# Attention by pairs of heads: probabilities times values on two halves of the array

## The chip, the cores and the metric

The kernel runs on one core of a Trainium2 chip. The metric is the time of one execution on the device in microseconds. The numbers of the profile come from one execution that the hardware profiler recorded. TensorE (PE) executes one queue in order: its matmuls appear as PE, its weight loads as PEld. VectorE is DVE, ScalarE is ACT, GpSimd is POOL, and SP issues the DMAs.

## The reference

Two layers work on 512 latent tokens and 256 context tokens, model width 1024. A layer is a half-step SwiGLU feed-forward, then four groups of heads side by side (a convolution, a linear recurrence, RWKV-7 in both directions, and attention), a joint output projection, and a second feed-forward half-step. Cut to the attention group, it computes this:

```python
def mla_mixer(u, uc, need_ctx_out, q_norm, w_uq, kv_norm, w_ukv, cos, sin):
    # q, k: 4 heads of 64 + 32 rotary columns; v: 4 heads of 64 columns
    k_all = jnp.concatenate([k, k_c], axis=1)      # 512 latent + 256 context keys
    v_all = jnp.concatenate([v, v_c], axis=1)
    def attend(q, k, v):
        s = jnp.einsum('bqhd,bkhd->bhqk', q, k, preferred_element_type=jnp.float32) * SM_SCALE
        p = jax.nn.softmax(s, axis=-1).astype(v.dtype)
        return jnp.einsum('bhqk,bkhd->bqhd', p, v)
    o = lax.map(lambda qb: attend(qb, k_all, v_all), q_blocks)   # blocks of 128 queries
    if need_ctx_out:
        o_c = attend(queries(uc), k_c, v_c)        # context attends to context alone
```

The last layer needs no context output.

## The kernel before

Everything is kept transposed, features on the 128 partitions and tokens along the free axis. The program is written as Python generators that emit instructions. A planner then orders each engine's queue: it takes instructions by priority (mostly the order in which they are emitted) as soon as its own model of time has their inputs ready, and less urgent work, above all the feed-forward matmuls of `gemm` (L503), fills what is left. The queues are fixed when the program is built; at run time each engine goes through its own in order and waits on semaphores. Tiles with one tag share a number of slots (`bufs`), and a slot is used again when the last reader of its old content is done.

`mla` (L886) emits the attention. It runs four times: for the context in layer 0 (`out` true, two blocks of 128 queries, two key tiles), for the latent tokens in layer 0 and in layer 1 (four blocks, six key tiles), and for the context in layer 1, where only keys and values are made. For each of four heads, one after the other, it makes the keys `kT` (L910 to L912, whose rotary part GpSimd copies) and the queries `qT` (L919 to L925); for each block of queries it makes the scores (L936, L938), the softmax (L941 to L945), the transposes of the probabilities in groups of three (L950), their copies into `pt` (L951), and the products with the values (L953), which are accumulated in one PSUM bank `po` for two heads: the even head writes partitions 0 to 63, the odd head 64 to 127. The tags `kT`, `qT` and `p` have two slots each, `pt` has one. After two heads, `split` (L514) writes `po` as the two parts that the output projection reads.

For the context and for the latent pass of layer 0, the steps of `mla` are dealt out alternately with those of `lru`, the linear recurrence (`merge`). In layer 1's latent pass attention runs as a whole beside the RWKV pipeline, and `lru` follows it. RWKV takes chunks through four stages: elements, the inverse of a triangular matrix in many small GpSimd instructions (L1171 to L1177), its composition from blocks (`rw_lev`), and the chain over chunks (`rw_chain`, L1242), which ends in readouts:

```python
for p, H in PH if need_y else []:      # H: partitions 0-63, then 64-127
    nc.tensor.matmul(py[H, p * 64:p * 64 + 64], sv[:, p, H], wr[:, p * 2 + c, 1, H], ...)      # L1279
for p, H in PH if need_y else []:
    nc.tensor.matmul(py[H, p * 64:p * 64 + 64], uv[H, p, H], lq[H, p * 2 + c, 1, :], ...)      # L1281
```

`rstd` (L418) spreads a column over 128 partitions; with two groups it goes through the two halves of the partitions in turn:

```python
for b in range(nb):
    for i in range(G):
        nc.tensor.matmul(ps[i * w:(i + 1) * w, b * 128:(b + 1) * 128], r[...].to_broadcast([128, w]), self.ident, ...)   # L435
```

Of the kernel before, what the change touches and what calls it, by code (L numbers as in the profile page):

```python
# [9 lines left out]
F32 = mybir.dt.float32  # L10
F32R = mybir.dt.float32r
AF = mybir.ActivationFunctionType
ALU = mybir.AluOpType
# [11 lines left out]
SM_SCALE = 96.0 ** -0.5  # L25
# [154 lines left out]
class Net:  # L180
# [705 lines left out]
    def mla(self, l, S, wp, yp, out, pr):  # L886
        nc, V, N = self.nc, self.nc.vector, S.n
        g = pr["g"]
        isx = S.i == 0
        nb = N // 128  # L890
        rp = self.c[:, C_RP:C_RP + 512]
        wkv = wp.tile([128, 4, 2, 64], F32, name=self.nm("wkv"))
        nc.sync.dma_start(out=wkv, in_=self.ins["ukv_w"][l])
        if out:
            wuq = wp.tile([128, 8, 128], F32, name=self.nm("wuq"))
            nc.sync.dma_start(out=wuq[:, :, 0:96], in_=self.ins["uq_w"][l].rearrange("p k h c -> p (k h) c"))
            self.rotcols(wuq[:, :, 64:128])

        vt = wp.tile([128, 4, 256], F32, name=self.nm("vt")) if isx else self.vtc
        for b in range(nb):  # L900
            ps = self.pM()
            nc.tensor.matmul(ps[:, 0:256], self.ckv[:, b * 128:(b + 1) * 128], wkv[:, :, 1, :], start=True, stop=True)
            nc.scalar.copy(out=vt[:, b, :], in_=ps[:, 0:256])
        vals = [vt[:, b, :] for b in range(nb)] + ([self.vtc[:, b, :] for b in range(2)] if isx else [])
        nk = len(vals)
        ys = []
        for h in range(4):
            kT = wp.tile([96, N], F32, tag="kT", name=self.nm("kT"), bufs=2) if isx else self.kTc[:, h, :]
            ps = self.pM()
            nc.tensor.matmul(ps[0:64, 0:N], wkv[:, h, 0, :], self.ckv, start=True, stop=True)  # L910
            nc.scalar.copy(out=kT[0:64], in_=ps[0:64, 0:N])
            nc.gpsimd.tensor_copy(out=kT[64:96], in_=self.kr)  # L912
            yield
            if not out:
                continue
            qT = wp.tile([96, N], F32, tag="qT", name=self.nm("qT"), bufs=2)
            ps = self.pM()
            for k in range(2):
                nc.tensor.matmul(ps[:, 0:N], wuq[:, k * 4 + h, :], self.cq[k], start=(k == 0), stop=(k == 1))  # L919
            if isx:  # L920
                nc.scalar.copy(out=qT[0:64], in_=ps[0:64, 0:N])
                t1 = wp.tile([128, nk * 128], F32, tag="p", name=self.nm("r1"), bufs=2)[:, 0:N]
                V.tensor_tensor(out=qT[64:96], in0=ps[64:96, 0:N], in1=rp[64:96], op=ALU.mult)
                V.tensor_tensor(out=t1[64:96], in0=ps[96:128, 0:N], in1=rp[96:128], op=ALU.mult)
                V.tensor_tensor(out=qT[64:96], in0=qT[64:96], in1=t1[64:96], op=ALU.add)  # L925
            else:
                nc.scalar.copy(out=qT, in_=ps[0:96, 0:N])
            n = nk * 128
            r = (h % 2) * 64
            if h % 2 == 0:  # L930
                po = self.pM() if self.wide else self.pC()
            for qb in range(nb):
                pt = wp.tile([128, nk, 128], F32, tag="pt", name=self.nm("pt"), bufs=1)
                ps = self.p2()
                q = qT[:, qb * 128:(qb + 1) * 128]
                nc.tensor.matmul(ps[:, 0:N], q, kT, start=True, stop=True)  # L936
                if isx:
                    nc.tensor.matmul(ps[:, N:n], q, self.kTc[:, h, :], start=True, stop=True)  # L938
                st = wp.tile([128, 4], F32, tag="st", name=self.nm("st"), bufs=4)
                p = wp.tile([128, n], F32, tag="p", name=self.nm("p"), bufs=2)  # L940
                V.tensor_reduce(out=st[:, 0:1], in_=ps[:, 0:n], axis=mybir.AxisListType.X, op=ALU.max)  # L941
                V.tensor_scalar(out=st[:, 1:2], in0=st[:, 0:1], scalar1=-SM_SCALE, scalar2=None, op0=ALU.mult)
                nc.scalar.activation(out=p, in_=ps[:, 0:n], func=AF.Exp, scale=SM_SCALE, bias=st[:, 1:2], accum_out=st[:, 2:3])
                V.reciprocal(out=st[:, 3:4], in_=st[:, 2:3])
                V.tensor_scalar(out=p, in0=p, scalar1=st[:, 3:4], scalar2=None, op0=ALU.mult)  # L945
                for k0 in range(0, nk, 3):
                    kn = min(3, nk - k0)
                    pp = self.pM()
                    for k in range(kn):
                        nc.tensor.transpose(pp[:, k * 128:(k + 1) * 128], p[:, (k0 + k) * 128:(k0 + k + 1) * 128], self.ident)  # L950
                    nc.scalar.copy(out=pt[:, k0:k0 + kn, :], in_=pp[:, 0:kn * 128].rearrange("p (k q) -> p k q", k=kn))  # L951
                for k in range(nk):
                    nc.tensor.matmul(po[r:r + 64, qb * 128:(qb + 1) * 128], vals[k][:, h * 64:(h + 1) * 64], pt[:, k, :], start=(k == 0), stop=(k == nk - 1))  # L953
                yield
            if h % 2:
                yt = self.ysplit(S, yp, 2)
                self.split(yt, po, N)
                ys.append(yt)
        self.my = ys


# [456 lines left out]
```

## Time and profile before

| | |
|---|---|
| median of three runs | 3392.51 us |
| lowest and highest of them | 3391.83, 3399.7 us |
| the profiled execution: its time, its span | 3401.43, 3399.7 us |
| mean granted clock of TensorE | 0.972 of full speed |
| attention, context, layer 0 | about 440 to 545 us |
| attention, latent, layer 0 | about 1040 to 1240 us |
| attention, latent, layer 1 | about 2730 to 2912 us |

A row of the chain of waits names an engine, a tile, a line and how many records were merged. An idle time is put down to the instruction that released the engine last. A tile's shape such as 128*64 after a matmul is that of its weights: 128 rows by 64 columns; behind it stands the moving tile.

### The profile page before, as it was taken

Reading aid. Unit: us, or ns where it says so; the run is one execution under the profiler, and the core shown is the slowest. Engines: PE = TensorE matmul, PEld = TensorE weight load, DVE = VectorE, ACT = ScalarE, POOL = GpSimd, SP = SyncE. Lnnn points to the kernel's source line nnn. Section 1 sums busy time; section 2 is a strip of 40 time slices with the busy share of each in tenths; the row PEclk is TensorE's granted clock in tenths of the full one; section 3 lists DMA queues with packets and bytes.
Section 4 is the critical chain, followed back from the end, with each engine's and each line's share of the span. In section 5 each row is a group of like instructions: output and inputs, shape, how many; then the busy total and the mean of one; then the engine's idle time right before and its main releaser. Section 6 shows DMA issues by size and latency. Waiting matters only on the chain.

```text
span 3399.7 us, 52623 instructions
## 1 busy us (share of the span) xinstructions
PE 3207.9 (94%) x20670; PEld 2598.6 (76%) x20670; DVE 2027.2 (60%) x3437; ACT 1383.2 (41%) x2364; POOL 961.9 (28%) x1205
## 2 busy tenths in 40 slices
PE   7999999999898999899999999999999889899998
PEld 3798866777776789688987778878888656578887
DVE  4555853554797565985676644543348977563335
ACT  3444553233536443444556332332235234642223
POOL 0222301351331123783212521211114266011111
PEclk9999999999999999899999999999999899899999
DMA  9665554432223454344544334233332251133232
GB/s 333 201 184 185 158 160 154 133 88 88 84 70 114 124 162 127 86 117 129 151 137 130 83 88 134 64 118 94 98 103 86 65 139 30 31 122 100 93 99 81
DMA packets 203544, 403.43 MB, mean 119 GB/s; under 512 B 97569, under 2 KB 103201, under 8 KB 203297
## 3 DMA queue, kind: packets, MB, share of 16 engines
q1 hardware_dynamic: 203296, 400.07, 38.8%
q8 instruction: 163, 2.67, 0.3%
q14 instruction: 85, 0.69, 0.1%
HBM read 392.39 MB, written 7.61 MB: 118 GB/s over the span
## 4 chain that ended last, share of the span: by engine, by line
PE 76%; DVE 13%; ACT 3%; issue 3%; DMA 2%; POOL 2%; SPq 0%; DVEq 0%; ACTq 0%; POOLq 0%
PE pg L503 60%; DVE ac L829 3%; PE pg L380 2%; PE pt L503 2%; DVE wlo L494 1%; PE pm L1119 1%; PE pm L380 1%; PE pt L936 1%; PE pc L953 1%; ACT whi L490 1%; DVE nacc L448 1%; PE pm L503 1%; POOL bt L1176 1%; PE pm L1220 1%; POOL bz L1177 1%
## 5 line engine op out<-in xcount | busy, mean ns | idle before, releaser
L503 PE MATMUL pg<-h,whi 128*128 128x256 f32 (+1 forms) x6128 | 1209.9, 345 | 17.8 <-ACT h L466 8.3
L503 PEld LDWEIGHTS pg<-h,whi 128*128 128x128 f32 x6128 | 976.1, 191 | 199.6 <-issue 30.3
L494 POOL TENSOR_TENSOR wlo<-raw,whi 128x1024 fp32r<-128x1024 f32 (+1 forms) x234 | 537.0, 2296 | 1997.4 <-ACT whi L490 1213.0
L490 ACT CAST whi<-raw 128x1024 fp32r<-128x1024 f32 (+1 forms) x621 | 607.3, 980 | 1073.5 <-PE pg L503 847.6
L494 DVE TENSOR_TENSOR wlo<-raw,whi 128x1024 fp32r<-128x1024 f32 (+1 forms) x387 | 449.7, 1163 | 403.6 <-PE pg L503 197.7
L503 PE MATMUL pg<-h,wlo 128*128 128x256 f32 (+1 forms) x3064 | 632.2, 344 | 6.7 <-DVE wlo L494 4.6
L503 PE MATMUL pg<-hid,whi 128*128 128x256 f32 (+1 forms) x2688 | 548.6, 340 | 19.6 <-DVE hid L517 5.4
L503 PEld LDWEIGHTS pg<-h,wlo 128*128 128x128 f32 x3064 | 492.0, 190 | 91.2 <-issue 16.3
L503 PEld LDWEIGHTS pg<-hid,whi 128*128 128x128 f32 x2688 | 425.8, 193 | 93.2 <-issue 11.2
L503 PE MATMUL pg<-hid,wlo 128*128 128x256 f32 (+1 forms) x1344 | 289.6, 334 | 3.0 <-POOL wlo L494 2.2
L522 DVE SCALAR_TENSOR_TENSOR x<-pg,msc,x 128x512 f32<-128x512 f32 (+1 forms) x232 | 155.2, 674 | 187.7 <-PE pg L503 186.5
L503 PEld LDWEIGHTS pg<-hid,wlo 128*128 128x128 f32 x1344 | 218.4, 193 | 27.9 <-POOL wlo L494 2.3
L517 DVE TENSOR_TENSOR hid<-ft,hid 128x512 fp32r<-128x512 f32 (+1 forms) x154 | 139.3, 905 | 60.7 <-ACT hid L516 60.3
L516 ACT CAST hid<-ft 128x512 fp32r<-128x512 f32 (+1 forms) x154 | 81.3, 528 | 220.9 <-DVE ft L552 220.6
L552 DVE SCALAR_TENSOR_TENSOR ft<-pg,ft 128x512 f32<-128x512 f32 (+1 forms) x152 | 86.8, 571 | 130.1 <-PE pg L503 129.2
L829 DVE SCALAR_TENSOR_TENSOR ac<-z,dw,ac 128x512 f32<-128x512 f32 (+1 forms) x180 | 142.2, 831 | 1.3
L551 DVE SCALAR_TENSOR_TENSOR ft<-ft,pg 128x512 f32<-128x512 f32 (+1 forms) x152 | 86.2, 567 | 90.9 <-ACT ft L550 90.5
L1177 POOL TENSOR_TENSOR bz<-bz,bt 32x14 f32<-32x14 f32 (+6 forms) x336 | 114.1, 340 | 23.8
L1176 POOL TENSOR_TENSOR bt<-bu,bz 32x14 f32<-32x14 f32 (+6 forms) x336 | 107.2, 319 | 22.9
L550 ACT ACTIVATE ft<-pg 128x512 f32<-128x512 f32 (+1 forms) x152 | 76.5, 503 | 71.5 <-PE pg L503 71.0
L522 DVE SCALAR_TENSOR_TENSOR ctx<-pg,msc,ctx 128x256 f32<-128x256 f32 x144 | 68.2, 480 | 49.4 <-PE pg L503 47.3
L466 ACT ACTIVATE h<-nt,mod 128x256 fp32r<-128x256 f32 x136 | 63.8, 503 | 74.7 <-DVE nt L465 74.4
(356 smaller groups left out, 3371.5 us busy)
## 6 DMA issues: line engine op xcount, KB each, us to landing
raw<-in_ffn_w_dram SPq DMA_DIRECT2D x456, 512.0 KB, 3.6
aw<-in_ada_w_dram SPq DMA_DIRECT2D x72, 512.0 KB, 5.6
raw<-in_ada_w_dram SPq DMA_DIRECT2D x72, 512.0 KB, 3.9
raw<-in_w_in_dram SPq DMA_DIRECT2D x65, 512.0 KB, 3.6
raw<-in_w_out_dram SPq DMA_DIRECT2D x56, 256.0 KB, 2.8
raw<-in_ffn_w_dram SPq DMA_DIRECT2D x40, 256.0 KB, 2.8
dl<-lq SPq DMA_DIRECT2D x48, 64.0 KB, 2.2
xt<-dz SPq DMA_DIRECT2D x48, 64.0 KB, 2.4
```

The source lines that it names most:

```text
L380: nc.tensor.matmul(pa[j * 32:(j + 1) * 32, :], self.cT[:, k, :], w[:, (j % 2) * 512:(j % 2) * 512 + 512], start=(k == 0), stop=(k == 7))
L490: nc.scalar.copy(out=hi[:, 0:n], in_=raw[:, 0:n])
L494: eng.tensor_tensor(out=lo[:, 0:n], in0=raw[:, 0:n], in1=hi[:, 0:n].bitcast(F32), op=ALU.subtract)
L503: self.nc.tensor.matmul(seg(ps[0:m, 0:N], s), W[w][:, k, c0:c0 + m], seg(hs[k][:, q, 0:N], s), start=(first and i == 0), stop=(last and i ...
L516: nc.scalar.copy(out=dst[:, 0, 0:N], in_=src[:, 0:N])
L517: nc.vector.tensor_tensor(out=dst[:, 1, 0:N], in0=src[:, 0:N], in1=dst[:, 0, 0:N].bitcast(F32), op=ALU.subtract)
L522: self.nc.vector.scalar_tensor_tensor(out=x, in0=seg(ps[:, 0:S.n], s), scalar=gate(m, S.i), in1=x, op0=ALU.mult, op1=ALU.add)
L551: nc.vector.scalar_tensor_tensor(out=t, in0=t, scalar=1.0, in1=pg[:, 0:N], op0=ALU.add, op1=ALU.mult)
L552: nc.vector.scalar_tensor_tensor(out=t, in0=pu[:, 0:N], scalar=0.5, in1=t, op0=ALU.mult, op1=ALU.mult)
L829: V.scalar_tensor_tensor(out=ac, in0=z, scalar=w, in1=ac, op0=ALU.mult, op1=ALU.add)
L1176: nc.gpsimd.tensor_tensor(out=tt, in0=u.u[:, I, k:k + 1].to_broadcast([32, n, m]), in1=z[:, k:k + 1, J].to_broadcast([32, n, m]), op=ALU.mult)
L1177: nc.gpsimd.tensor_tensor(out=z[:, I, J], in0=z[:, I, J], in1=tt, op=ALU.subtract)
```

## The change

The loop over four heads becomes a loop over two pairs. Keys and queries of both heads are made first. For each block of queries, both heads go through scores, softmax and transposes into a `pt` of their own (two slots), and then the products of the two heads alternate, key tile by key tile. The generator also yields after each head's transposes and after the products.

```diff
-        for h in range(4):
-            kT = wp.tile([96, N], F32, tag="kT", name=self.nm("kT"), bufs=2) if isx else self.kTc[:, h, :]
...
-            yield
-            if not out:
-                continue
-            qT = wp.tile([96, N], F32, tag="qT", name=self.nm("qT"), bufs=2)
...
+        for h0 in (0, 2):
+            kTs, qTs = [], []
+            for h in (h0, h0 + 1):
+                kT = wp.tile([96, N], F32, tag="kT", name=self.nm("kT"), bufs=2) if isx else self.kTc[:, h, :]
...
+                kTs.append(kT)
+                yield
+                if not out:
+                    continue
+                qT = wp.tile([96, N], F32, tag="qT", name=self.nm("qT"), bufs=2)
...
+                qTs.append(qT)
             if not out:
                 continue
-            r = (h % 2) * 64
-            if h % 2 == 0:
-                po = self.pM() if self.wide else self.pC()
+            po = self.pM() if self.wide else self.pC()
             for qb in range(nb):
-                pt = wp.tile([128, nk, 128], F32, tag="pt", name=self.nm("pt"), bufs=1)
...
+                pts = []
+                for h, kT, qT in zip((h0, h0 + 1), kTs, qTs):
+                    pt = wp.tile([128, nk, 128], F32, tag="pt", name=self.nm("pt"), bufs=2)
...
+                    pts.append(pt)
+                    yield
+
                 for k in range(nk):
-                    nc.tensor.matmul(po[r:r + 64, qb * 128:(qb + 1) * 128], vals[k][:, h * 64:(h + 1) * 64], pt[:, k, :], start=(k == 0), stop=(k == nk - 1))
+                    for r, pt in zip((0, 64), pts):
+                        h = h0 + r // 64
+                        nc.tensor.matmul(po[r:r + 64, qb * 128:(qb + 1) * 128], vals[k][:, h * 64:(h + 1) * 64], pt[:, k, :], start=(k == 0), stop=(k == nk - 1))
                 yield
-            if h % 2:
-                yt = self.ysplit(S, yp, 2)
-                self.split(yt, po, N)
-                ys.append(yt)
+            yt = self.ysplit(S, yp, 2)
+            self.split(yt, po, N)
+            ys.append(yt)
```

The instructions between (scores, softmax, transposes, copies) are the same as before, one loop deeper.

## Rows read from the trace of the kernel before

**Rows 1.** The page, part 1, busy us, share of the span and instructions.
```profile
PE 3207.9 (94%) x20670; PEld 2598.6 (76%) x20670; DVE 2027.2 (60%) x3437; ACT 1383.2 (41%) x2364; POOL 961.9 (28%) x1205
```

**Rows 2.** The page, part 4, shares of the chain that ended last, by engine.
```profile
PE 76%; DVE 13%; ACT 3%; issue 3%; DMA 2%; POOL 2%; SPq 0%; DVEq 0%; ACTq 0%; POOLq 0%
```

**Rows 3.** Windows: length, busy us (instructions) of PE, PEld, DVE, ACT, POOL; clock, DMA share, GB/s.
```profile
440.00:545.00 105.00, 103.11 (x463) 70.35 (x462) 44.41 (x95) 48.97 (x91) 9.57 (x4) 1.00 0.40 119
1040.00:1240.00 200.00, 192.63 (x1273) 153.23 (x1273) 121.83 (x187) 105.89 (x171) 30.95 (x14) 0.99 0.41 125
2730.00:2912.00 182.00, 166.83 (x1894) 112.37 (x1890) 127.93 (x317) 82.56 (x233) 106.10 (x292) 0.97 0.28 68
```

**Rows 4.** Instructions of L953: records, ns (min/median/max), first and last start.
```profile
L953 PE MATMUL pc<-pt,vt x128: 272/273/324, 1064.6 to 1236.3; 128*64 128x128 f32 x128
...
L953 PE MATMUL pg<-pt,vt x128: 272/273/323, 2754.1 to 2908.8; 128*64 128x128 f32 x128
...
L953 PE MATMUL pc<-pt,vtc x96: 272/273/323, 462.0 to 1236.8; 128*64 128x128 f32 x96
...
L953 PE MATMUL pg<-pt,vtc x64: 272/273/273, 2755.0 to 2909.2; 128*64 128x128 f32 x64
```

**Rows 5.** The chain in order of time, 2895 to 2930: start us, us, what.
```profile
2898.99 1.46 PE pg L953 x12
...
2902.25 0.59 PE pm L435 x8
2902.83 1.31 PE pg L953 x12
```

**Rows 6.** The chain in order of time, 1575 to 1600.
```profile
1595.98 0.38 PE pc L1275 x8
1596.37 0.23 PE pc L1279 x8
1596.60 0.38 PE pc L1281 x8
```

**Rows 7.** The chain in order of time, 440 to 545.
```profile
462.07 0.58 PE pc L953 x4
```

**Rows 8.** Timeline of TensorE, 1555 to 1563: start us, us, engine, line, operation, records.
```profile
1557.61 0.45 PE L1266 MATMUL pc<-w,xt 64*64 64x64 f32 x8
...
1560.65 0.45 PE L1275 MATMUL pc<-uv,bk 128*64 128x64 f32 x8
1560.93 0.40 PE L1279 MATMUL pc<-wr,su 128*64 128x64 f32 x8
```

**Rows 9.** Groups of instructions, 2730 to 2912: busy us, mean ns, idle before and releaser.
```profile
L1177 POOL TENSOR_TENSOR bz<-bz,bt 32x14 f32<-32x14 f32 (+6 forms) x112 | 32.9, 294 | 7.6
L1176 POOL TENSOR_TENSOR bt<-bu,bz 32x14 f32<-32x14 f32 (+6 forms) x112 | 31.8, 284 | 7.7
...
L951 ACT COPY pt<-pg 128x384 f32<-128x384 f32 x32 | 14.3, 480 | 15.0 <-PE pg L950 13.6 <-PE pg L953 1.3
```

**Rows 10.** Timeline of GpSimd, 2785 to 2800.
```profile
2793.14 0.86 POOL L912 COPY kT<-kr 32x512 f32<-32x512 f32 x1
```

**Rows 11.** TensorE's waits, 1040 to 1240: us in total, times, longest; first and last of six.
```profile
PE pt L936 <- DVE qT L925: 3.8, 3, 2.0
...
PE pg L503 <- DVE ctx L522: 0.2, 1, 0.2
```

**Rows 12.** Waits of all engines, 1043 to 1237.
```profile
ACT pt L951 <- PE pm L950: 15.9, 7, 5.4
```

**Rows 13.** The chain's shares by line, 1040 to 1240 and 2730 to 2912.
```profile
by line: PE pg L503 45.3%; PE pc L953 12.0%; PE pt L936 7.1%; PE pm L950 5.3%; PE pg L380 4.9%; PE pm L861 3.5%; PE pt L938 3.4%; PE pm L919 2.8%; DVE qT L925 2.5%; DVE wlo L494 1.2%; PE pm L910 1.2%; ACT whi L490 1.0%; DVE ti L867 1.0%; PE
...
by line: PE pg L953 9.9%; PE pt L936 6.2%; issue 6.0%; PE pm L1119 5.7%; PE pg L950 4.8%; PE pg L380 4.2%; PE pm L1220 3.3%; PE pg L919 3.1%; ACT p L943 2.7%; DVE bx L1109 2.6%; PE pt L938 2.6%; DMA aw<-in_ada_w_dram 2.4%; DMA xx<-dz 2.1%; 
```

**Rows 14.** TensorE's waits, 2730 to 2912, first and last of 18.
```profile
PE pg L380 <- DMA aw<-in_ada_w_dram: 3.7, 3, 1.9
...
PE pm L1119 <- POOL bz L1177: 0.2, 1, 0.2
```

More of the change, by code (lines that the diff above doesn't have):

```diff
@@ L906, in mla @@
         ys = []
-        for h in range(4):
-            kT = wp.tile([96, N], F32, tag="kT", name=self.nm("kT"), bufs=2) if isx else self.kTc[:, h, :]
[L909 to L912, printed above, removed]
-            yield
+        for h0 in (0, 2):
+            kTs, qTs = [], []
+            for h in (h0, h0 + 1):
+                kT = wp.tile([96, N], F32, tag="kT", name=self.nm("kT"), bufs=2) if isx else self.kTc[:, h, :]
+                ps = self.pM()
+                nc.tensor.matmul(ps[0:64, 0:N], wkv[:, h, 0, :], self.ckv, start=True, stop=True)
+                nc.scalar.copy(out=kT[0:64], in_=ps[0:64, 0:N])
+                nc.gpsimd.tensor_copy(out=kT[64:96], in_=self.kr)
+                kTs.append(kT)
[3 more added lines that the diff above has]
+                qT = wp.tile([96, N], F32, tag="qT", name=self.nm("qT"), bufs=2)
+                ps = self.pM()
+                for k in range(2):
+                    nc.tensor.matmul(ps[:, 0:N], wuq[:, k * 4 + h, :], self.cq[k], start=(k == 0), stop=(k == 1))
+                if isx:
+                    nc.scalar.copy(out=qT[0:64], in_=ps[0:64, 0:N])
+                    t1 = wp.tile([128, nk * 128], F32, tag="p", name=self.nm("r1"), bufs=2)[:, 0:N]
+                    V.tensor_tensor(out=qT[64:96], in0=ps[64:96, 0:N], in1=rp[64:96], op=ALU.mult)
+                    V.tensor_tensor(out=t1[64:96], in0=ps[96:128, 0:N], in1=rp[96:128], op=ALU.mult)
+                    V.tensor_tensor(out=qT[64:96], in0=qT[64:96], in1=t1[64:96], op=ALU.add)
+                else:
+                    nc.scalar.copy(out=qT, in_=ps[0:96, 0:N])
+                qTs.append(qT)
@@ L914, in mla @@
             if not out:
                 continue
-            qT = wp.tile([96, N], F32, tag="qT", name=self.nm("qT"), bufs=2)
[L917 to L927, printed above, removed]
@@ L928, in mla @@
             n = nk * 128
-            r = (h % 2) * 64
-            if h % 2 == 0:
-                po = self.pM() if self.wide else self.pC()
+            po = self.pM() if self.wide else self.pC()
             for qb in range(nb):
-                pt = wp.tile([128, nk, 128], F32, tag="pt", name=self.nm("pt"), bufs=1)
[L934 to L951, printed above, removed]
@@ new lines, in mla @@
+                pts = []
+                for h, kT, qT in zip((h0, h0 + 1), kTs, qTs):
+                    pt = wp.tile([128, nk, 128], F32, tag="pt", name=self.nm("pt"), bufs=2)
+                    ps = self.p2()
+                    q = qT[:, qb * 128:(qb + 1) * 128]
+                    nc.tensor.matmul(ps[:, 0:N], q, kT, start=True, stop=True)
+                    if isx:
+                        nc.tensor.matmul(ps[:, N:n], q, self.kTc[:, h, :], start=True, stop=True)
+                    st = wp.tile([128, 4], F32, tag="st", name=self.nm("st"), bufs=4)
+                    p = wp.tile([128, n], F32, tag="p", name=self.nm("p"), bufs=2)
+                    V.tensor_reduce(out=st[:, 0:1], in_=ps[:, 0:n], axis=mybir.AxisListType.X, op=ALU.max)
+                    V.tensor_scalar(out=st[:, 1:2], in0=st[:, 0:1], scalar1=-SM_SCALE, scalar2=None, op0=ALU.mult)
+                    nc.scalar.activation(out=p, in_=ps[:, 0:n], func=AF.Exp, scale=SM_SCALE, bias=st[:, 1:2], accum_out=st[:, 2:3])
+                    V.reciprocal(out=st[:, 3:4], in_=st[:, 2:3])
+                    V.tensor_scalar(out=p, in0=p, scalar1=st[:, 3:4], scalar2=None, op0=ALU.mult)
+                    for k0 in range(0, nk, 3):
+                        kn = min(3, nk - k0)
+                        pp = self.pM()
+                        for k in range(kn):
+                            nc.tensor.transpose(pp[:, k * 128:(k + 1) * 128], p[:, (k0 + k) * 128:(k0 + k + 1) * 128], self.ident)
+                        nc.scalar.copy(out=pt[:, k0:k0 + kn, :], in_=pp[:, 0:kn * 128].rearrange("p (k q) -> p k q", k=kn))
+                    pts.append(pt)
+                    yield
```

## The prediction

> **What bounds the kernel now.** I read the page's busy times first [rows 1], then the chain that ended last [rows 2], and then cut out the three stretches in which attention runs [rows 3]. TensorE is busy 94% of the span and is 76% of the chain, so the first question for any edit is how much TensorE issue time it takes away; the second is whether TensorE in that stretch was the engine that the others waited for. The stretches differ in this. In the context pass (440 to 545 us) TensorE is busy 103.1 of 105 us, and in layer 0's latent pass (1040 to 1240) 192.6 of 200: what attention leaves free is filled with feed-forward matmuls (L503). In layer 1's latent pass (2730 to 2912) it is 166.8 of 182, the filler is the RWKV pipeline, and GpSimd is busy 106 us there [rows 3].
>
> The matmuls that the change touches are those of L953, probabilities times values. Each matmul of the program is two records, since 416 records [rows 4] stand for 208 matmuls: 4 heads x 2 blocks x 2 key tiles = 16 in the context pass and 4 x 4 x 6 = 96 in each of two latent passes. All have 64 columns of weights and a moving tile of 128 columns.
>
> In the chain, which lays instructions end to end, 12 such records (one head, one block) take 1.46 us, but 1.31 us when they follow another group with 64-column weights [rows 5]. So a record costs 1.31 / 12 = 0.109 us, and entering the form costs 0.15 us. The same 0.15 us shows a second time: eight records of L1279 cost 0.23 us right behind L1275, while L1275, which enters the form, and L1281, which leaves it, take 0.38 us [rows 6]. The four records of a block in the context pass take 0.58 us [rows 7], which is 4 x 0.109 + 0.15.
>
> **What a pair on two halves costs.** The row nearest to the new form is L435: 64-column weights, 128 moving columns, consecutive matmuls on alternating halves of one bank. Eight records take 0.59 us [rows 5]; less the 0.15 that is 0.055 us a record, half of L953's. L1279 alternates as well, with a different moving tile for each half as the pair will have, and its 0.23 / 8 = 0.029 us for 64 columns is the same rate again [rows 6]. So two halves run side by side in this kernel already, whether they share the moving operand or not.
>
> A rule of the Trainium skill speaks against this: the page "TensorE: Matmul & The Clock Gate", Part 3 (packing small matmuls), says that a weight load overlaps a running matmul only where the row group differs, and both halves of a pair use all 128 rows. By that rule the pair would save nothing and the sum below would be zero. The 0.055 us of L435 disagrees with it, and I go by the row.
>
> **The change, part by part.**
>
> *Interleaved products.* Before, a pair of heads and a block cost 2 x 1.46 = 2.92 us; after, 24 x 0.055 + 0.15 = 1.47, so 1.45 less. A latent pass has 2 pairs x 4 blocks = 8 of these, 11.6 us; two passes give 23.2. In the context pass 2 x 0.58 becomes 8 x 0.055 + 0.15 = 0.59, four times 0.57, 2.3 us. Together 25.5 us of TensorE time. The other end: if the entry cost scaled with the group, 24 x 0.59 / 8 = 1.77, a pair saves 1.15, and the sum is 16 x 1.15 + 2.3 = 20.7. I take the first, since the 0.15 shows in two forms.
>
> *Does the order survive the planner?* The first head's products could be issued as soon as its probabilities are there, long before the second head's, and then no pair would stand side by side. What speaks against it is how it treats one bank: L1279's inputs are those that L1260 used, yet L1279 does not go ahead of L1275 in the same bank; between L1266 and L1275 it puts 3 us of other work, and L1279 comes right behind L1275 [rows 8]. Both heads of a pair write one bank, so I expect first, second, first, second. At most the leading matmul of the first head goes alone, which costs one more entry, 0.15 us in each of 20 pairs, 3 us as a bound.
>
> *Products moved back, probabilities in two buffers.* The first head's products now wait for the second head's softmax. Nothing reads them before the pair's end (the split), where the second head was last anyway: nothing on the path. With one buffer the copies of L951 had to wait for the products before them; that wait is 1.3 us in all of layer 1's stretch [rows 9], off ScalarE's 82.6 busy of 182, so I give the second buffer nothing. The next block's copies wait for the pair's products as they waited for the single head's.
>
> *Both heads' keys and queries first.* The same instructions: per head three matmuls' worth of L910 and L919, copies on ScalarE and GpSimd, three rotary steps on VectorE. No DMA and no queue entry of SP moves. What is new is a wait: keys and queries have two slots, so the third head's copies, L912 on GpSimd among them, wait for the last scores of the first head, and the fourth's for those of the second. Before, a slot was a whole head old by then. Behind L912 on GpSimd stand the 224 small instructions of the RWKV triangular inverse in that stretch, 64.7 us [rows 9], and the chain waits for these. The copy itself is 0.86 us and has no wait ahead of it now [rows 10]. I price it at nothing, since the first head's last scores lie one head-block before the pair ends; its bounds are below.
>
> *More yields* (28 steps of attention for 20 in a latent pass) only change how the recurrence's six steps are dealt between; in layer 1's latent pass there is no dealing, and where no context output is needed the instructions stay as they were.
>
> **How much of it reaches the end.** Layer 0, latent: TensorE waits for 7.7 us in six rows of its waits, and the others wait for it (ScalarE 15.9 us for transposes alone) [rows 11, 12]; the products are 12.0% of the chain there, 24 us, which is all they take [rows 13]. So nearly all of 11.6 us counts; I take nine tenths, 10.4. Context: 2.3 us in a stretch with 2 us idle, nine tenths, 2.1. Layer 1: 9.9% of the chain, 18 us of about 23, is the products [rows 13]; that would give at most 0.77 x 11.6 = 8.9. But 14.6 us of TensorE's waits in 18 rows [rows 14] and GpSimd, VectorE and DMA pieces in the same chain say that a second path runs close behind; half, 5.8 us. Sum 10.4 + 2.1 + 5.8 = 18.3 us.
>
> The profiled execution took 3401.4 us (span 3399.7), 8.9 above the median of the three runs, 3392.5; so the sum gives 3383 for an execution like the profiled one and 3392.5 - 18.3 = 3374 for the median, which I predict. A change of 0.3%, 10.2 us, is about what can be told from none: faster ends at 3382.3, slower begins at 3402.7.
>
> **Rivals.**
>
> *Layer 1 swallows it.* If the RWKV pipeline sets the pace there, layer 1 gives nothing, and if layer 0's freed time half turns into waits for VectorE (busy 121.8 of 200), 5.8 + 2.1 = 7.9 us are left: 3384.6. For it: VectorE, GpSimd and DMA pieces in layer 1's chain. Against it: layer 0's waits go the other way [rows 12].
>
> *The halves do not run side by side, or the pairs are torn apart* by other work in the queue: each record keeps 0.109 us, at best an entry of 0.15 us is saved 20 times, 3 us, 3389.5. Against it stand L435 and L1279 [rows 5, 6], which do run side by side; for it, that no row here shows two different moving tiles of 128 columns on the two halves. This is also where the page's rule would lead.
>
> *Slower: GpSimd held up by the keys.* In layer 1, L912 for heads three and four is put in GpSimd's queue before its slot is free, with the inverse's chain behind it. One head-block is 182 / 16 = 11.4 us; two waits of one and a half each are 34 us. Less the 12.5 of the other two stretches that is +21.6: 3414. It decides from 2 x 11.4 us on, where the loss (22.8) exceeds the 12.5 by 10. Against it: GpSimd's copy goes in right as its slot comes free now (2793.14) [rows 10], and the planner knows the slot.
>
> **How the numbers follow.** Forecast 0.58, layer 1 swallows it 0.16, no overlap 0.12, slower 0.14. The planner writes all queues anew, which no row prices; TensorE's waits in layers 0 and 1, 22 us, may shrink or grow by half of that, 11 us. The forecast's own range is then 25.5 + 11 below to 7.9 less 3 below the median: 3356 to 3388. To leave out no more than 2 in 10 the range goes on over the two small-gain rivals to 3396. Faster: 0.54 of the forecast and 0.06 of the first rival, 0.60. Slower: 0.12, most of the last rival. Same: 0.28.
>
> **What would show it.** Groups of L953 with 24 records at 1.4 to 1.8 us in the chain (2.9 refutes the overlap), eight such in each latent pass; attention in layer 0 about 10 us shorter with TensorE still above 93% busy; in layer 1 some 6 us shorter, with TensorE's waits up by about as much. The prediction is wrong if groups of 12 or fewer records of one head remain, if GpSimd shows idle time ahead of L912, or if a stretch without attention changes by over 10 us.

## The result and the profile after

The changed kernel takes 3357.72 us (median, 3355.87 to 3359.95) where the kernel before took 3392.8 beside it: a ratio of 0.9893, 95% interval 0.9875 to 0.991, 35 us less. Measured a second time the ratio was 0.9882 (0.9865 to 0.99).

The profiled execution of before that stands above lay 9 us over its median. A second one, 3393.45 us with a span of 3391.7, is an ordinary one; below, "before" in traces is that second execution. The changed kernel's profiled execution has a span of 3353.9 us.

Four landmarks cut both traces into stretches: the last column sum of the norm ahead of layer 0's second feed-forward (L406, `pm<-nacc`), the last step of layer 1's convolution taps (L829), the last column sum of layer 1's third norm (L406, `pt<-nacc`), and the last one of all (`pg<-nacc`). Records with their durations in ns and their first and last start, first of before, then of the changed kernel, whose lines from the products on are later by 10 or 11 (L953 is L964, L1281 is L1291):

```profile
L406 PE MATMUL pg<-nacc,on x26: 377/484/796, 23.1 to 3381.9; 128*128 128x256 f32 x26
...
L406 PE MATMUL pm<-nacc,on x8: 377/378/483, 322.9 to 1733.0; 128*128 128x256 f32 x8
...
L406 PE MATMUL pt<-nacc,on x4: 379/504/634, 2998.2 to 3010.5; 128*128 128x256 f32 x4
...
L829 DVE SCALAR_TENSOR_TENSOR ac<-z,dw,ac x180: 467/739/2936, 388.4 to 2693.9; 128x512 f32<-128x512 f32 x120, 128x256 f32<-128x256 f32 x60
...
L953 PE MATMUL pg<-pt,vtc x64: 272/273/273, 2749.2 to 2901.1; 128*64 128x128 f32 x64
...
L1281 PE MATMUL pc<-lq,uv x320: 217/219/367, 712.1 to 2919.6; 64*64 64x64 f32 x160
```

```profile
L406 PE MATMUL pg<-nacc,on x26: 377/483/797, 23.0 to 3344.1; 128*128 128x256 f32 x26
...
L406 PE MATMUL pm<-nacc,on x8: 377/379/483, 322.3 to 1719.9; 128*128 128x256 f32 x8
...
L406 PE MATMUL pt<-nacc,on x4: 379/559/796, 2953.7 to 2972.6; 128*128 128x256 f32 x4
...
L829 DVE SCALAR_TENSOR_TENSOR ac<-z,dw,ac x180: 467/739/2936, 387.7 to 2679.5; 128x512 f32<-128x512 f32 x120, 128x256 f32<-128x256 f32 x60
...
L964 PE MATMUL pg<-pt,vtc x64: 272/273/323, 2752.2 to 2855.3; 128*64 128x128 f32 x64
...
L1291 PE MATMUL pc<-lq,uv x320: 218/218/366, 690.5 to 2919.7; 64*64 64x64 f32 x160
```

Up to layer 0's norm the changed kernel is 13.1 us ahead (1733.0, 1719.9). From there to the taps nothing changes (960.9, 959.6), and from layer 1's third norm to the end nothing either (371.4, 371.5). Between taps and third norm of layer 1, 316.6 us become 293.1, 23.5 less. So the smaller part comes from layer 0 and the context, the larger from layer 1, which is the opposite of what was forecast (12.5 and 5.8 us); the two kernels below that change one layer alone agree. The shares themselves are uncertain: two traces of one kernel differ by up to 9 us at the norm (before: 1741.8 and 1733.0) and 4 us in layer 1's stretch (changed: 293.1 and 297.0).

**The pairs.** The chain that ended last, layer 0:

```profile
1155.48 0.36 PE pc L964 x2
...
1165.02 1.46 PE pc L964 x22
...
1171.07 0.36 PE pc L964 x2
...
1175.35 1.45 PE pc L964 x22
```

The first head's leading matmul (two records) goes alone, 4 to 10 us early, and the other 22 records go together at 1.46 us, which is what the 12 records of one head alone took [rows 5]. That is 1.82 us for a pair and block where two groups of 12 took 2.92. In layer 1, where other matmuls stand between, two of the eight pairs have their 22 records in one piece; most others are in two, such as 12 and 10:

```profile
2767.35 0.81 PE pg L964 x12
...
2770.49 0.80 PE pg L964 x10
...
2825.74 1.45 PE pg L964 x22
```

Summed over the kernel from each group's start to the next start on TensorE, the products took 52.4 us before and 33.3 after, 19.1 less.

**The stretches.** Windows of the changed kernel (length, busy us of PE, PEld, DVE, ACT, POOL, clock, DMA share, GB/s): attention in layer 0, layer 1's stretch, attention in it, and what comes right behind attention there.

```profile
1040.00:1200.00 160.00, 157.36 (x1100) 123.12 (x1100) 107.37 (x167) 94.54 (x154) 23.98 (x12) 1.00 0.42 130
...
2679.50:2972.60 293.10, 261.76 (x2406) 176.90 (x2405) 214.91 (x496) 148.22 (x367) 133.18 (x319) 0.92 0.31 85
2740.00:2858.00 118.00, 111.88 (x1452) 77.63 (x1450) 90.00 (x229) 61.65 (x175) 83.40 (x229) 1.00 0.24 53
2858.00:2912.00 54.00, 49.12 (x462) 33.48 (x458) 36.94 (x74) 37.59 (x75) 7.02 (x17) 0.78 0.15 37
```

The same of before, layer 1's stretch and the 48 us right behind attention, and then, before and after, the whole way from attention's last product to the third norm:

```profile
2693.90:3010.50 316.60, 274.69 (x2425) 189.67 (x2424) 215.73 (x488) 155.78 (x371) 133.29 (x320) 0.92 0.29 80
2905.00:2953.00 48.00, 32.51 (x150) 21.06 (x147) 29.76 (x56) 36.00 (x55) 1.30 (x1) 0.72 0.08 22
...
2901.10:3010.50 109.40, 85.72 (x453) 65.11 (x452) 66.72 (x120) 60.92 (x106) 14.66 (x12) 0.84 0.24 73
```
```profile
2855.30:2972.60 117.30, 102.53 (x780) 76.08 (x778) 76.36 (x156) 62.62 (x131) 19.03 (x33) 0.84 0.24 71
```

In layer 1's stretch TensorE was idle 41.9 us before (316.6 - 274.7) and 31.3 after; it was busy 12.9 us less, of which 9.4 are the products. What moved is attention's place. Its last product lies 207.2 us behind the taps before (2901.1 - 2693.9) and 175.8 after, 31.4 sooner, while RWKV's last readouts (L1281, L1291) come later, 225.7 us behind the taps before (2919.6) and 240.2 after (2919.7). So attention went ahead of RWKV's work, and some of that work was left for later. Before, RWKV had 18.5 us to go when attention ended; the recurrence and the convolution, which follow attention, then ran with little beside them, TensorE busy 32.5 of 48 us at a granted clock of 0.72. After, RWKV has 64.4 us to go, and TensorE is busy 49.1 of 54 in the same place, at 0.78. From attention's last product to the third norm the way is 7.9 us longer than before (117.3, 109.4), but TensorE idles 14.8 us of it in place of 23.7. So 8.9 of the 10.6 us of idle time that went away lie behind attention. During attention little changed: TensorE's own waits were 14.6 us in 18 rows of the first trace over 182 us [rows 14], 8.7 us in the second one over 154 us (2748 to 2902), and are 5.9 us in nine rows over 118 us here, of which the longest are:

```profile
PE pm L1230 <- DVE st L948: 1.8, 1, 1.8
PE pm L1230 <- ACT su L1216: 0.9, 1, 0.9
PE pc L1270 <- ACT yt L1299: 0.9, 1, 0.9
```

GpSimd's copy of the keys (L914, before L912 [rows 10]) shows no wait ahead of it. GpSimd's timeline, fourth head of layer 1:

```profile
2794.76 0.60 POOL L1186 TENSOR_TENSOR bt<-bu,bz 32x50 f32<-32x50 f32 x1
2795.42 0.60 POOL L914 COPY kT<-kr 32x512 f32<-32x512 f32 x1
2796.10 0.37 POOL L1187 TENSOR_TENSOR bz<-bz,bt 32x50 f32<-32x50 f32 x1
```

### The profile page after: what moved, and what is told of

The parts are those of the page before. It is cut to its first block, busy times and chain, and to the rows that moved or that the text cites. A ratio compares the mean times of both kernels' runs of the same rounds, so it can differ in the third digit from the quotient of the medians.

```text
span 3353.9 us, 52657 instructions
## 1 busy us (share of the span) xinstructions
PE 3181.5 (95%) x20670; PEld 2575.3 (77%) x20670; DVE 2019.0 (60%) x3437; ACT 1379.2 (41%) x2360; POOL 960.9 (29%) x1205
## 4 chain that ended last, share of the span: by engine, by line
PE 49%; DVE 10%; POOL 3%; ACT 2%; issue 2%; DMA 1%; SPq 0%; POOLq 0%; DVEq 0%; ACTq 0%
PE pg L503 40%; PE pt L503 1%; DVE ac L829 1%; PE pm L503 1%; DVE nacc L448 1%; POOL bz L1187 1%; POOL bt L1186 1%; DVE h L467 1%; DVE nt L465 1%; DVE wlo L494 1%; PE pg L380 1%; PE pm L1129 1%; PE pm L1230 1%; PE pt L942 1%; ACT whi L490 1%
## 5 line engine op out<-in xcount | busy, mean ns | idle before, releaser
L503 PE MATMUL pg<-h,whi 128*128 128x256 f32 (+1 forms) x6128 | 1206.9, 345 | 10.1 <-ACT whi L490 4.5
L503 PEld LDWEIGHTS pg<-h,whi 128*128 128x128 f32 x6128 | 973.1, 190 | 195.5 <-issue 34.8
L503 PE MATMUL pg<-h,wlo 128*128 128x256 f32 (+1 forms) x3064 | 625.6, 343 | 2.1 <-POOL wlo L494 2.1
L503 PE MATMUL pg<-hid,whi 128*128 128x256 f32 (+1 forms) x2688 | 544.1, 339 | 17.4 <-DVE ft L552 4.6
L503 PEld LDWEIGHTS pg<-h,wlo 128*128 128x128 f32 x3064 | 491.1, 190 | 80.7 <-issue 12.9
L503 PEld LDWEIGHTS pg<-hid,whi 128*128 128x128 f32 x2688 | 423.8, 192 | 84.0 <-issue 7.7
L503 PE MATMUL pg<-hid,wlo 128*128 128x256 f32 (+1 forms) x1344 | 288.8, 334 | 1.0 <-DVE wlo L494 1.0
L503 PEld LDWEIGHTS pg<-hid,wlo 128*128 128x128 f32 x1344 | 216.9, 191 | 26.1 <-DVE wlo L494 1.2
L829 DVE SCALAR_TENSOR_TENSOR ac<-z,dw,ac 128x512 f32<-128x512 f32 (+1 forms) x180 | 144.0, 840 | 1.2
L466 ACT ACTIVATE h<-nt,mod 128x256 fp32r<-128x256 f32 x136 | 64.4, 504 | 82.7 <-DVE nt L465 82.7
```

The source lines that it names most:

```text
L503: self.nc.tensor.matmul(seg(ps[0:m, 0:N], s), W[w][:, k, c0:c0 + m], seg(hs[k][:, q, 0:N], s), start=(first and i == 0), stop=(last and i ...
L829: V.scalar_tensor_tensor(out=ac, in0=z, scalar=w, in1=ac, op0=ALU.mult, op1=ALU.add)
```

## The experiments

Theory: the halves run side by side, and the TensorE time that this saves comes off the end nearly one for one. As this alone is too little for 35 us, a second part was looked for. Its candidates: two heads in the softmax at once (latency), the second `pt` buffer by itself, or a lucky order of the queues.

All results, with ratios to before on the same chip. The products' time is the sum over TensorE as above; "norm" is the landmark of layer 0; the last three columns are layer 1's: attention's last product behind the taps, the stretch from taps to third norm, and TensorE's idle time in it.

| kernel | median us | ratio (95%) | products | norm | attention ends | stretch | idle |
|---|---|---|---|---|---|---|---|
| before (second trace) | 3393.45 | | 52.4 | 1733.0 | 207.2 | 316.6 | 41.9 |
| second `pt` buffer alone | 3396.33 | 1.0006 (0.9998 to 1.0015) | 53.8 | 1740.9 | 204.8 | 311.5 | 36.0 |
| pairs, context and layer 0 | 3386.07 | 0.9975 (0.9966 to 0.9985) | 43.3 | 1722.4 | 214.9 | 323.4 | 44.3 |
| pairs, layer 1 | 3380.36 | 0.9939 (0.9923 to 0.9954) | 42.5 | 1742.5 | 180.1 | 299.2 | 36.0 |
| second head first | 3379.3 | 0.9952 (0.9936 to 0.9967) | 27.6 | 1727.6 | 186.3 | 308.1 | 40.0 |
| head by head | 3369.18 | 0.9925 (0.9909 to 0.9941) | 42.0 | 1723.4 | 187.2 | 303.4 | 36.8 |
| head by head, alternated in its queues | 3366.39 | 0.99 (0.9883 to 0.9916) | 30.1 | 1720.0 | 188.6 | 303.2 | 35.9 |
| changed, two runs in its queues | 3373.95 | 0.9928 (0.9913 to 0.9943) | 44.9 | 1729.7 | 182.8 | 300.6 | 30.0 |
| changed, three runs in its queues | 3364.96 | 0.9894 (0.9878 to 0.9911) | 37.7 | 1722.9 | 178.4 | 295.3 | 30.8 |
| changed, one `p` buffer in layer 1 | 3361.96 | 0.9899 (0.9883 to 0.9914) | 33.4 | 1719.8 | 187.1 | 296.3 | 33.9 |
| changed, three `p` buffers in layer 1 | 3358.62 | 0.988 (0.9863 to 0.9898) | 33.4 | 1719.8 | 175.4 | 291.6 | 31.1 |
| changed | 3357.72 | 0.9893 (0.9875 to 0.991) | 33.3 | 1719.9 | 175.8 | 293.1 | 31.3 |
| changed, again | 3357.05 | 0.9882 (0.9865 to 0.99) | 33.7 | 1719.3 | 179.8 | 297.0 | 29.6 |

**Head by head, and the second head first.** Two kernels change only the order in which a pair's products are emitted.

```diff
-for k in range(nk):
-    for r, pt in zip((0, 64), pts):
+for r, pt in ((64, pts[1]), (0, pts[0])):      # head by head
+    for k in range(nk):
```
```diff
 for k in range(nk):
-    for r, pt in zip((0, 64), pts):
+    for r, pt in ((64, pts[1]), (0, pts[0])):  # second head first
```

> The changed kernel, but the twelve products of a pair are issued head by head, the second head's six first and then the first head's six, so that they still stand together behind the second head's transposes and only the alternation is gone. If the gain is the two halves running side by side, a pair costs 24 x 0.109 + 0.15 = 2.8 us instead of the 0.36 + 1.46 = 1.82 us that the changed kernel's chain shows: 16 pairs x 0.95 and some 2 us in the context pass are lost, 3375 us (ratio to the kernel before about 0.995). If the gain comes from the second buffer and the order by pairs, with the overlap worth little, it stays at 3358 within 4 us (0.990).

> The changed kernel with the alternation begun by the second head, so that no product can go ahead alone: one group of 24 records instead of 2 and 22. By the overlap theory a pair costs 24 x 0.06 + 0.15 = 1.6 us for 1.82, 16 x 0.24 = 4 us less: 3354 us. By the theory that the order of the pairs matters and not the matmuls' time, no difference beyond 4 us either way.

Chains that ended last, of the first and of the second:

```profile
1112.26 2.38 PE pc L964 x24
...
1155.30 0.80 PE pc L964 x6
...
1156.89 1.73 PE pc L964 x18
```
```profile
2832.59 0.81 PE pg L964 x12
...
2847.40 0.81 PE pg L964 x12
...
2849.27 0.81 PE pg L964 x12
```

Of the second, a pair in one piece, in TensorE's timeline:

```profile
1106.06 1.09 PE L964 MATMUL pc<-pt,vt 128*64 128x128 f32 x16
1106.99 0.61 PE L964 MATMUL pc<-pt,vtc 128*64 128x128 f32 x8
1107.52 1.13 PE L942 MATMUL pt<-kT,qT 96*128 96x512 f32 x2
```

The rates are as the theory has them: 24 records take 2.38 us (or 0.80 and 1.73) head by head. When the pair begins with the head that is ready last, so that nothing goes ahead alone, they take 1.62 us in two pieces of 12 and 1.46 in one (1107.52 - 1106.06), no more than the 22 of the changed kernel. The times don't follow. The first lies between the two expected (3375 and 3358), the second misses both. With only 10.4 us of products saved the first is 25 us faster than before, and the second, which saves 24.8 of them, gains 16. The planner writes all queues anew for each, and against the changed kernel's second trace the second is 11 us longer in layer 1's stretch (308.1, 297.0) and 8 us later at layer 0's norm, with less time in products than it. Hence two needs: find where the gain beyond the products is made, and compare side by side with the queues held still.

**The buffer, and the two layers apart.**

```diff
-pt = wp.tile([128, nk, 128], F32, tag="pt", name=self.nm("pt"), bufs=1)
+pt = wp.tile([128, nk, 128], F32, tag="pt", name=self.nm("pt"), bufs=2)   # in the kernel before
```
```diff
-m = self.mla(l, S, mp, yp, out, pr)
+m = (self.mla_single if self.wide else self.mla)(l, S, mp, yp, out, pr)      # pairs in context and layer 0
+m = (self.mla_single if not self.wide else self.mla)(l, S, mp, yp, out, pr)  # the other kernel: layer 1
```

(`mla_single` is the function before, `self.wide` is true in layer 1's latent pass.)

> The kernel before with two buffers for the transposed probabilities and nothing else. If the overlap makes the gain, at most the 1.3 us of ScalarE's wait in layer 1 and a few us of other order: 3388 to 3396 us (0.999 to 1.001). If the second buffer makes it, because a head's copies need not wait for the products of the head before, at least half of the 35 us: 3375 us or less (0.995), with layer 1's attention shortened from 160 us towards the 105 us of the changed kernel.

> Pairs in the context pass and in layer 0's latent pass only; layer 1's latent pass as before. By the prediction's sum layer 0 and the context give 12.5 of 18.3 us, some two thirds of the gain: 3370 us (0.993). If layer 1 is where the unexpected part of the gain came from (the two profiles differ by 27 us of 46 there), only 12 to 18 us remain: 3375 to 3380 us (0.995 to 0.996).

> Pairs in layer 1's attention alone; the context and layer 0 as before, head by head with one buffer. Pairs in the context and layer 0 alone gave 8.5 us (as much as their products saved on TensorE, 8.8). Theory 1 with the latency part (pairs let two heads' softmax go on at once, layer 1's attention ends some 50 us earlier, and the recurrence and the convolution, which wait a lot, then run beside RWKV): the rest of the gain is made here, 35 - 8.5 = 26 us, so 3367, and the stretch from the taps to the third norm of layer 1 takes 293 to 300 us in place of 319.5. Rival (only the products count, the rest is luck of the queues): the products of layer 1, 9.6 us, so 3384, with the queues' luck anywhere between 3375 and 3395.

The buffer alone does nothing (1.0006). Pairs in the context and layer 0 give 8.5 us (5 to 12 by the interval), less than either expectation and about what their products save, 9.1. The agreement is loose: in the trace the norm comes 10.6 us sooner than in the second trace of before, and layer 1's stretch, whose code is as before, is 6.8 us longer. Pairs in layer 1 give 0.61% of 3393, 20.7 us (16 to 26), where their products save 9.7 (23.9 to 14.2); the stretch, 299.2, is as the first theory expected. So a part beyond the products, some 11 us here, is made in layer 1, and the two kernels add up to 29 of the 35 us. The six that are missing lie within the intervals.

**Alternation undone or made in queues that stay.** Here (edits condensed) the program was planned as it is, and only then the matmuls of a latent pair changed places among themselves on TensorE; every other instruction keeps its place in its queue. Behind the leading matmul the changed kernel has b a b a b ... (a the first head); the context's pairs stay.

```diff
+for g in groups:                  # the places of one pair's 12 products
+    a, b = [ins[n] for n in g[0::2]], [ins[n] for n in g[1::2]]
+    new = b[:3] + a[1:] + b[3:]   # three runs
+    new = a[1:] + b               # the other kernel: two runs
+    for n, i in zip(g[1:], new):
+        ins[n] = i
```
```diff
+    b, a = [ins[n] for n in g[:6]], [ins[n] for n in g[6:]]   # in the queues of head by head
+    for n, i in zip(g, [i for two in zip(b, a) for i in two]):
+        ins[n] = i
```

> The changed kernel with every engine's queue as planned for it; only afterwards, inside the places that a latent pair's products hold on TensorE, the order becomes three of the second head, five of the first, three of the second (the leading product of the first head stays where it is; the context's pairs stay). Nothing else moves, so this is the price of running the halves side by side, without new queues. In the changed kernel 22 such records take 1.45 us; one head after the other they took 2.38 us for 24 in the kernel with head-by-head products, so a pair should take some 2.2 us, 0.75 more, 12 us for 16 pairs. Theory 1 (the halves side by side count nearly one for one): 3357.7 + 12 = 3370, within 3367 to 3373. Rival 2 (layer 1 waits for other things, only layer 0's half counts): 3364. Rival 3 (the gain of 35 us came from the queues that the planner wrote, the overlap is swallowed by waits): 3358 to 3360.

> The kernel with head-by-head products (3369.2 us), its queues kept; only afterwards the two heads' products change places inside their own pair so that they alternate, the second head first. Products took 42.0 us of TensorE time in that kernel and 27.6 us where full groups of 24 records alternate, so 13 to 14 us less are to be had. Theory 1 (counts nearly one for one): 3369.2 - 12 = 3357, within 3354 to 3361. Rival 2 (only layer 0's half counts): 3362 to 3363. Rival 3 (the queues made the gain, overlap swallowed): 3367 to 3371.

> The changed kernel with its queues kept, as the kernel with the alternation undone, but now in two runs only: behind the leading product the five others of the first head, then all six of the second, so that only one change of halves is left in a pair (three runs left two of them and cost 1.79 us where the alternation costs 1.45). From the kernel with head-by-head products (2.38 us for 24 records) a pair should cost about 2.1 us for the 22 records, 0.65 more than alternated, 10 us for 16 pairs, half in each layer. Theory 1 (the halves side by side count nearly one for one where TensorE sets the pace): 9 us over the changed kernel on the same chip, between 6 and 12; in the trace some 5 us by the norm of layer 0 and 4 us more by the third norm of layer 1. Rival (overlap swallowed by waits, the queues made the gain): within 2 us of the changed kernel.

> The changed kernel once more, as the base on the same chip for the two kernels beside it: a ratio to before of 0.989, as in its first measurement (0.9875 to 0.991).

Chains that ended last, of three runs and of two runs:

```profile
1150.27 1.79 PE pc L964 x22
...
1165.87 1.79 PE pc L964 x22
```
```profile
1107.80 2.17 PE pc L964 x22
...
1152.12 2.17 PE pc L964 x22
```

Three runs undid less than I had reckoned: 1.79 us in place of 1.46, and 4.0 us over the kernel (37.7 less 33.7) in place of 12. The time shows nothing of it (0.9894 beside 0.9893 and 0.9882), nor could it, at intervals of 6 us to either side. So that kernel decided nothing, and the two runs were made: 2.17 us each, 11.2 us more over the kernel. On one chip they took 3373.95 us and the changed kernel 3357.05. By the ratios, 0.9928 less 0.9882, that is 0.46% or 15.6 us, and 8 to 23 by both intervals (0.0015 and 0.00175, added as squares). The rival by which waits swallow the overlap, within 2 us, falls. In the traces 10.4 us of it have come by layer 0's norm and 3.6 more in layer 1's stretch (products 5.0 and 6.2 us); the second is no more than two traces of one kernel differ by, so what the overlap is worth in layer 1 by itself isn't settled.

Alternating the queues of head by head saved 11.9 us of products and, across two chips, 0.25% or 8.5 us, uncertain by nearly as much. Against before on the chip of head by head that would be 3361 us, the edge of the first theory's range; the rivals are within the uncertainty, so only the sign agrees. In its trace layer 1 gained nothing although its products took 6.3 us less. TensorE's busy time there is the same all the same (266.6, 267.3), and the granted clock, 0.93 in the first kernel's stretch and 0.90 in the second's, is what likely covers it:

```profile
2680.30:2983.70 303.40, 266.59 (x2403) 182.66 (x2402) 215.38 (x495) 150.11 (x368) 133.46 (x319) 0.93 0.29 82
```
```profile
2679.90:2983.10 303.20, 267.30 (x2406) 180.87 (x2404) 213.94 (x495) 151.00 (x368) 133.61 (x319) 0.90 0.29 82
```

**More and less room for the softmax in layer 1.** If layer 1 gains because attention ends sooner, a kernel in which it ends later should lose.

```diff
-p = wp.tile([128, n], F32, tag="p", name=self.nm("p"), bufs=2)
+p = wp.tile([128, n], F32, tag="p", name=self.nm("p"), bufs=3 if self.wide else 2)
+p = wp.tile([128, n], F32, tag="p", name=self.nm("p"), bufs=1 if self.wide else 2)   # the other kernel
```

> The changed kernel with three instead of two buffers for the probabilities before their transposes, in layer 1's attention alone. No work changes. Latency theory (layer 1's attention is a chain of waits, the sooner it ends the more of the recurrence and the convolution is hidden under RWKV): attention there takes under 105 us and the stretch from the taps to the third norm of layer 1 under 293 us, by some 5 us, so about 3353. Rival (only the products' time on TensorE counts): 3357 to 3359. Rival (luck of the queues): any value within 15 us of 3358, without relation to the length of attention.

> The changed kernel with one buffer in place of two for the probabilities before their transposes, in layer 1's attention alone: the two heads of a pair can no longer be in the softmax at once, while the products still alternate on two halves. No work is added. Latency theory (layer 1's stretch, from the taps to the third norm, ends some 115 us after attention's last product, so what counts there is how soon attention ends): attention's last product, 176 us after the taps in the changed kernel, comes at 190 to 210, and the stretch of 293 us becomes 303 to 320, so 3368 to 3385. Rival (only TensorE time counts; the products' time is unchanged): within 4 us of the changed kernel. Rival (luck of the queues): a stretch whose length has nothing to do with attention's end, say 293 to 300 with the end at 200 or the reverse.

A third buffer changes nothing, attention's end included (175.4), so the latency theory's 3353 missed. With one buffer attention ends 7.3 us later than in the changed kernel beside it (187.1, 179.8), less than expected, and the stretch is no longer (296.3, 297.0); the medians differ by 5 us, inside the intervals. Between pairs and single heads the stretch goes with attention's end (175 to 189 with 292 to 308, 205 to 215 with 312 to 323); among the kernels with pairs it does not. So this one missed: the stretch came out as the rival of the queues' luck has it, and the rule "so much behind attention's end" is too simple. The kernel shows one thing more. With one buffer the second head's probabilities have to wait until the first head's are transposed, and attention still ends 20 us sooner than before (187.1, 207.2). So having both heads' probabilities at once explains at most part of attention's earlier end.

**The kernel before, profiled again.**

> The kernel before, profiled a second time, since its first profiled execution lay 8.9 us above the median of its runs. Expected where the first trace was ordinary: the norm of layer 0 at 1741 to 1743 us, the stretch from the taps to the third norm of layer 1 at 311 to 324 us, and some 5 to 9 us less in all than in the first trace. If instead the first trace was odd in one of these two stretches, that one is shorter by as much.

Its layer 1 stretch (316.6) is as expected, but the norm came at 1733.0, not 1741.8: the first trace's excess lay in layer 0. It isn't peculiar to that execution, as two other kernels with the old code there have 1740.9 and 1742.5; every kernel with pairs in layer 0 lies between 1719.3 and 1729.7.

## Why the prediction was right, and where not

*The number.* 3374 us were forecast, with a range from 3356, and 3357.72 came: 35 us of gain for 18.3, inside the range by 1.7 us. That it is inside is partly luck. The low end was put together from all 25.5 us of products and 11 us of luck with the queues; what came was 19.1 us of products and some 16 us beyond them.

*What a pair costs.* Right in kind and in size: two halves of 128*64 weights with different moving tiles go side by side, and a full group of 24 records takes 1.46 us, as forecast (1.47). The Trainium skill's page "TensorE: Matmul & The Clock Gate", Part 3, by which weight loads overlap a running matmul only where row groups differ, would have it otherwise, and the measurement decides against it here. The sum was too large. The prediction named the leading matmul alone as a bound of 0.15 us an entry; in fact it is the rule and costs 0.36 us, with nothing saved behind it, since the 22 records that are left take as long as 24. So a pair takes 1.82 us and not 1.47. 25.5 us were forecast and 19.1 came, below the low end of 20.7.

*How much reaches the end.* The nine tenths of layer 0 and the context hold as far as the interval tells: pairs there alone gave 8.5 us (5 to 12) for 9.1 of products. With the queues kept, 11.2 us of products in both layers were worth 15.6 (8 to 23). The rivals in which the halves don't overlap, or in which waits swallow all of it, are refuted by this, and the one by which layer 1 gives nothing by the kernel with pairs in layer 1 alone.

*The step that failed* is the price of nothing that the prediction gave to all of the change but the products (both heads' keys first, two `pt` buffers, products held back). It asked only what the products' time was worth in layer 1, "half, 5.8 us", and expected TensorE's waits there to rise. Pairs in layer 1 alone gave 20.7 us (16 to 26) for 9.7 us of products, and TensorE's idle time in the stretch fell, from 41.9 us to 36.0 in that kernel and to 31.3 and 29.6 in the changed one. Attention there became 48 us shorter, not 6 (first to last product 152.8 us before, 105.1 after). That more than half of it comes with little of the overlap is shown by the kernel head by head (stretch 303.4) and by the two runs (300.6), with products only 4.4 and 2.9 us shorter there than before. Whether "half" was right for the products themselves is open, as said above.

What pairs do is let attention end 19 to 32 us nearer to the taps, in whatever order their products go, with RWKV's work left for the time of the recurrence and the convolution. That this leftover fills their waits is likely from the two windows but not shown, since across the kernels TensorE's idle time behind attention doesn't go with it: 23.7 us with 18.5 us of RWKV to go (before), 14.8 with 64.4 (changed), but 15.1 with 32.9 (the second `pt` buffer alone) and 20.1 with 63.4 (pairs in layer 1 alone). Why attention gets ahead is open too: the second `pt` buffer by itself does not do it (204.8), nor does it need two `p` buffers (187.1).

The Trainium skill's page "Perfetto Trace Analysis", section "Optimization Strategy", says that stretches with different busiest engines may gain by being interleaved; the two windows behind attention, 32.5 busy of 48 and 49.1 of 54, are in line with it; no run here tests it by itself.

What stays open is how much of this second part is the pairs' structure and how much the order that the planner happened to write. For the structure: nine kernels with pairs in layer 1, in six different plans of the queues, all lie between 291.6 and 308.1, and the four traces without lie between 311.5 and 323.4. For the order: the kernel with the second head first saves most of the products and has the longest stretch of those nine, 16 us over the shortest, and one `p` buffer put attention's end later at no loss. The ±11 us that the prediction allowed for new queues fits the 20 us between those two emission orders, but is less than the 16 us that came beyond the products.

*The slow rival* did not come: no wait ahead of L914, whose copies in that stretch take 0.60 to 0.70 us.

*What would show it.* Attention in layer 0 ended 40 us sooner (its last product, L953 at 1231.9, L964 at 1191.9), not 10, with TensorE busy 157.4 of 160. TensorE's feed-forward matmuls (L503) from attention's first product to its last, and from there to the norm, before and after (length, PE, PEld, clock, DMA share, GB/s):

```profile
1061.40:1231.90 170.50, 102.02 (x722) 90.61 (x722) 1.00 0.39 121
1231.90:1733.00 501.10, 376.79 (x2664) 344.30 (x2665) 0.97 0.44 130
```
```profile
1061.30:1191.90 130.60, 78.83 (x556) 69.75 (x555) 1.00 0.40 123
1191.90:1719.90 528.00, 397.58 (x2837) 366.64 (x2837) 0.96 0.45 133
```

Less filler was done beside attention, 102.0 us before and 78.8 after; what was not done beside it came later, 20.8 us more. So 13 of the 40 us were left by the norm, and the stretch without attention grew by 27. By the prediction's own measure (no such stretch changes by over 10 us) its picture of layer 0's schedule was wrong, and so was that of eight groups of 24 records in each latent pass (none stood so), while the sum for it held within the interval.

## What to carry to other kernels

Products of 64 columns each on the two halves are worth pairing even with full rows, and the time comes off the end where TensorE is busy 96 to 98% of the stretch. A leading matmul that goes alone saves nothing; beginning with the head that is ready last avoids it, but here that kernel was 20 us slower than the changed one, with the queues planned anew. When an edit puts two independent chains in work at once, follow what comes behind them: in layer 1 TensorE lost 10.6 us of idle time beside 9.4 us of matmuls, and 8.9 of these lay in the next stage. With a planner that rewrites all queues, an edit's own price is measured only by changing the order after planning; otherwise two emission orders of the same work differ by 20 us.

## What was not expected of the hardware

In an alternating group the matmul on the other half added nothing to the time, and one without a partner cost as much as two: 22 records and 24 both take 1.46 us, 10 and 12 take 0.80 and 0.81, and the six matmuls of one head alone 1.46 [rows 5].

A single change of halves already hides much. The same 11 matmuls of a pair take 2.17 us with one change of halves, 1.79 with two and 1.46 with ten. All on one half they would take 2.55, an estimate from 0.218 us a matmul (two records of 0.109) and the 0.15; head by head the same estimate for 12 matmuls is 2.77, and 2.38 was measured. So the first and the second change are worth 0.38 us each, and the eight further ones only 0.33 together, since the time has then come down to what the six matmuls of one half take alone. Why one change hides that much, no run here separates.
